# Scale, shift and norm gain folded into two rows per routing, normalised rows kept for the residual, VectorE in place of GpSimd

## The chip, the core and the metric

The kernel runs on one core of a Trainium2 chip. Its engines are TensorE (PE, with a queue of its own for weight loads, PEld), VectorE (DVE), ScalarE (ACT), GpSimd (POOL) and SyncE (SP), which here only issues transfers; ACT and POOL issue some too. Each engine works through its own queue in order and waits on semaphores. The metric is the device time of one launch in microseconds (us), as the median of several runs.

## The reference

Two layers (DEPTH 2) run over 256 latent and 256 context tokens of width 1024; the second layer computes the latent tokens alone. What the change touches is the path from the token mixer's result to the second norm. Cut to that, for each token row:

```
mod = c @ w_ada + b_ada                       # six rows per layer: shift, scale, gate, shift2, scale2, gate2
x1  = layer_norm(alpha*x + gate*mix) * g1 + b1
h2  = x1 * (1 + scale2) + shift2
ffn = moe(h2) = routed experts(h2) + shared expert(h2)
x2  = layer_norm(alpha*x1 + gate2*ffn) * g2 + b2
```

The router takes sigmoid scores of h2 over 64 experts, keeps four groups of eight and the eight best experts of these, and each expert is a SwiGLU network of inner width 256. The shared expert has the same shape.

## The kernel before

Tokens lie in tiles of 128 rows by 1024: four tiles in layer 0, two in layer 1. Matmuls run on operands that are split in a high and a low half: `hilo` (L91, L92) has ACT write the high half and DVE subtract it for the low one (`hb`, `hTl`, `row`). For weights, `whi` is ACT's and `wlo` is DVE's, or POOL's for the share that `split_on_pool` asks for; `raw` is the loaded slab of 1 MB.

A layer has four stages. The **mixer** ends in the merged branches. The **routing** (about 822 to 972 us in layer 0, 2115 to 2229 in layer 1) begins with the out-projection w_o: per tile, matmuls, `yo` and `xr` (L1233, L1234: the gated result added to the residual), the statistics (L560, L561), a chain of tiny DVE instructions for the root (L577 to L583) and the normalised row tile (L570). PE then transposes the tile (L390), ACT applies scale and shift by column (L394), ACT and DVE split it (`hb`), PE computes router logits (L1093, L1094) and the shared expert, and DVE chooses the experts (L1097 to L1122). Beside this, `by_rows` makes the same rows without the transpose, for the experts: the norm's gain (L1182, DVE) and bias (L1183, POOL) give `x1`, which is written to DRAM as x1d; the scale (L1186, DVE) and the shift (L1187, POOL) give `h2`, which is written as h2d. Gain and bias come as two broadcast loads (lng, lnb), scale and shift as `mod` rows that `modulation` has written to DRAM. When the last tile is chosen, DVE writes the list of experts `eid` (L1263); SP reads it and issues the first expert weights w_exp (L129). The **expert stage** gathers rows of h2d and runs the experts. The **post stage** (`post`) loads the shared expert's result yd, the residual x1d, the gate `mod` (m = 5) and the experts' rows y8 on SP's queue; `base` (L1764, L1765) forms alpha*x1 + gate*yd per tile, L1780 to L1787 add the experts' sum, and the second norm follows.

In mixer and routing a scheduler sets the order on each engine: it places instructions by its own estimates of when each engine is free. The expert and the post stage are under `manual_schedule`: there the order is that of the code. In the routing of layer 0, slabs of w_out and w_shared share two `raw` buffers, so a slab can only be loaded when ACT and DVE have split the one two before it.

Of the kernel before, what the change touches and what calls it, by code (L numbers as in the profile page):

```python
# [11 lines left out]
F32 = mybir.dt.float32  # L12
# [3 lines left out]
AF = mybir.ActivationFunctionType  # L16
OP = mybir.AluOpType
# [4 lines left out]
D = 1024  # L22
T = 256
L = 2
# [46 lines left out]
def body(ctx, tc, A, out):  # L71
# [104 lines left out]
    ident = C("ident")  # L176
# [123 lines left out]
    def modulation(chunks, r):  # L300

        n = 2 * len(chunks)
        q = bank("aux", 2)[:, :2 * n].rearrange("p (a b) -> p a b", a=2)
        for i in range(2):
            pe.matmul(q[:, i], r[:, i * 128:i * 128 + 128], C("sel")[:, :n], start=True, stop=True)
        for i, (l, j) in enumerate(chunks):
            m, k0 = j // 4, 2 * (j % 4)
            dve.tensor_tensor(modT[:, l, m, k0:k0 + 2], q[:, :, 2 * i:2 * i + 2],
                              bT_ada[:, l, m, k0:k0 + 2, None].to_broadcast([128, 2, 2]), op=OP.add)
            done[l, m] = done.get((l, m), 0) + 1  # L310
            if m > 1 and done[l, m] == 4:
                p = bank("aux", 2)
                pe.transpose(p[:16, :128], modT[:, l, m].rearrange("p k w -> p (k w)"), ident)
                s = wk.tile([16, 128], F32, name="modr", tag="modr")
                act.activation(s, p[:16, :128], AF.Copy)
                act.dma_start(modrow[l, m].rearrange("w (k c) -> k w c", c=128), s)

    def ada(*chunks):

# [49 lines left out]
    def actt(name):  # L369
        return wk.tile([128, 512], F32, name=name, tag="act", bufs=3)  # L370

    def after_norm(l, m, ln):


        f = wk.tile([128, 2, 8, 2], F32, name="fuse", tag="fuse", bufs=1)
# [667 lines left out]
    def moe(l, merged, x_src):  # L1043
# [6 lines left out]
        with pool_of(f"moe{l}") as K, ExitStack() as es:  # L1050
# [122 lines left out]
                return up, down  # L1173


            gb, bb = bcast(Y, A["ln"][l, 0:1], "lng"), bcast(Y, A["ln"][l, 1:2], "lnb")
            rowm = {}

            def by_rows(t):
                if t % 2 == 0:  # L1180
                    rowm.update({m: mod_b(Y, l, m, t // 2) for m in (4, 3)})
                dve.tensor_tensor(xr[t], xr[t], gb, op=OP.mult)  # L1182
                pool.tensor_tensor(xr[t], xr[t], bb, op=OP.add)  # L1183
                act.dma_start(x1d[t * 128:t * 128 + 128], xr[t])
                h_ = Y.tile([128, D], F32, name="h2")
                dve.tensor_tensor(h_, xr[t], rowm[4], op=OP.mult)  # L1186
                pool.tensor_tensor(h_, h_, rowm[3], op=OP.add)  # L1187
                act.dma_start(h2d[t * 128:t * 128 + 128], h_)
                if gather:
                    hilo(*rowp[t], h_)  # L1190
# [10 lines left out]

            def shared(*tiles):
                if not steps:
                    with split_on_pool(1):
                        steps.extend(dense(A["w_shared"][l], lambda t, k: tuple(z[:, k] for z in h2T[t]), put))
                for t in tiles:
                    steps[0](t)
                    with split_on_pool(1):
                        steps[1](t)

            steps = []
# [538 lines left out]
            with pool_of(f"post{l}") as P:  # L1750
# [7 lines left out]
                if l + 1 < L:  # L1758
                    mod = after_norm(l + 1, 0, 4 * l + 2)

                def base(t):

                    f = sh[t // 2][:, t % 2]
                    dve.tensor_tensor(f, f, g5[t // 2], op=OP.mult)  # L1764
                    dve.scalar_tensor_tensor(xs[t], xs[t], ALPHA, f, op0=OP.mult, op1=OP.add)  # L1765
# [22 lines left out]
                    mv.append(stats(xs[t]))  # L1788
                    ys_.append(root(mv[t]))

                def gain_bias():
                    z = rows2()
                    for i in range(2):
                        sp.dma_start(z[:, i], A["ln"][l, 2 + i:3 + i].to_broadcast([128, D]))
                    return z[:, 0], z[:, 1]

                mv, ys_, yb = [], [], []
                with tc.manual_schedule():
                    if l + 1 < L:
                        w = load(A["w_in"][(l + 1) * 38 + S_RQ])  # L1800
                    for t in range(0, NT, 2):
                        sp.dma_start(sh[t // 2], yd[t * 128:t * 128 + 256].rearrange("(a p) d -> p a d", a=2))
                    for t in range(NT):
                        sp.dma_start(xs[t], x1d[t * 128:t * 128 + 128])
                    g5 = [mod_b(P, l, 5, w_, NS) for w_ in range(NS)]
                    if l + 1 == L:
                        gb, bb = gain_bias()
                    for t in range(NT):
                        base(t)
                    y8v = y8.rearrange("(t p i j) d -> t p i j d", p=128, i=4, j=2)  # L1810
# [2 lines left out]
                        for i in range(4):  # L1813
                            sp.dma_start(yb[t][i], y8v[t, :, i])
                    if l + 1 < L:
                        gb, bb = gain_bias()
                    ln_exp_set()
                    if l + 1 < L:
                        ready[l + 1, S_RQ] = w
# [154 lines left out]
```

## Time and profile before

| | us |
|---|---|
| median of 3 runs | 2800.93 |
| lowest and highest | 2794.92, 2804.31 |
| the profiled execution | 2791.87 |
| its span, first to last instruction | 2790.1 |
| PE busy | 2562.6 (92%) |
| DVE busy | 1645.9 (59%) |
| ACT busy | 1286.5 (46%) |
| POOL busy | 595.5 (21%) |
| mean granted TensorE clock | 0.964 of full |

The profile is that of one execution. "Busy" counts computing instructions alone; the time between an instruction's issue and its start is the idle time that the rows put in brackets, with the instruction that ended it behind the arrow. 1.8 us of the profiled execution's time lie around its span.

### The profile page before, as it was taken

To read this page: it belongs to the slowest core of one execution; us is meant where nothing else is said; L and a number is where in the kernel's file an instruction comes from. 1 tells how busy PE (TensorE), PEld (TensorE's weight loads), DVE (VectorE), ACT (ScalarE), POOL (GpSimd) and SP (SyncE) were. 2 spreads that over 40 slices of the span, in tenths; PEclk is the share of its full clock that TensorE was granted. 3 is DMA by queue.
4 is the path that set the end of the run, shared out by engine and by line. 5 is a ranking of instruction groups with operands and counts; after the bars stand their busy time and mean duration, and the time that the engine had idled before them with its cause. 6 is when DMAs were issued, how large, how long until landed. Compare 5 with 4: busy or idle time off the path is not lost. (4 is left out here: it accounts for less than half of the span.)

```text
span 2790.1 us, 39222 instructions
## 1 busy us (share of the span) xinstructions
PE 2562.6 (92%) x14587; PEld 1846.6 (66%) x14587; DVE 1645.9 (59%) x2968; ACT 1286.5 (46%) x2364; POOL 595.5 (21%) x418
## 2 busy tenths in 40 slices
PE   7999999999997899999999799998989799999995
PEld 6887777788777665555555378887888554554552
DVE  5698895258857654555554577886697622232224
ACT  3434425237852355555555355445475333343331
POOL 2443311222233311212221122213123200000000
PEclk9999999999998899999999899999999799999998
DMA  5221355621152499999999952255325499999996
GB/s 228 72 75 61 106 207 221 231 92 45 61 201 106 171 356 402 408 395 394 402 402 393 358 208 103 95 182 183 120 84 191 163 392 423 422 362 397 419 416 263
DMA packets 118900, 684.09 MB, mean 245 GB/s; under 512 B 21936, under 2 KB 24624, under 8 KB 45744
## 3 DMA queue, kind: packets, MB, share of 16 engines
q1 hardware_dynamic: 92544, 624.80, 57.2%
q0 software_dynamic: 20496, 41.98, 4.0%
q10 hardware_dynamic: 5664, 14.75, 1.4%
q8 instruction: 117, 1.92, 0.3%
q14 instruction: 79, 0.65, 0.1%
HBM read 651.76 MB, written 61.93 MB: 256 GB/s over the span
## 5 line engine op out<-in xcount | busy, mean ns | idle before, releaser
L91 ACT ACTIVATE whi<-raw 128x1024 fp32r<-128x1024 f32 x416 | 428.1, 1053 | 241.1 <-PE mm L231 122.3
L92 DVE TENSOR_TENSOR wlo<-raw,whi 128x1024 fp32r<-128x1024 f32 x305 | 382.8, 1276 | 194.2 <-ACT whi L91 191.0
L231 PE MATMUL mm<-whi,hb 128*128 128x256 f32 (+1 forms) x2016 | 409.6, 300 | 20.2 <-ACT whi L91 5.8
L92 POOL TENSOR_TENSOR wlo<-raw,whi 128x1024 fp32r<-128x1024 f32 x111 | 271.6, 2455 | 639.9 <-ACT whi L91 563.6
L231 PEld LDWEIGHTS mm<-whi,hb 128*128 128x128 f32 x2016 | 334.6, 199 | 28.0 <-issue 7.0
L1578 PE MATMUL mm<-raw,xw 128*64 128x512 f32 x1408 | 331.4, 600 | 0.6 <-DMA raw<-in_w_exp 0.6
L231 PE MATMUL mm<-hb,whi 128*128 128x512 f32 (+1 forms) x1152 | 326.1, 368 | 4.9 <-ACT whi L91 2.9
L231 PE MATMUL mm<-wlo,hb 128*128 128x256 f32 (+1 forms) x1008 | 299.9, 298 | 4.6 <-DVE wlo L92 3.9
L1648 POOL DMA_INDIRECT y<-y,ix x94 | 95.5, 1016 | 974.6 <-ACT y L1644 866.3
L606 DVE SCALAR_TENSOR_TENSOR cacc<-G,cpk,cacc 128x512 f32<-128x512 f32 (+1 forms) x464 | 287.4, 619 | 10.5
L231 PE MATMUL mm<-whi,xp 128*128 128x512 f32 x736 | 262.0, 410 | 1.7 <-ACT whi L91 1.7
L231 PEld LDWEIGHTS mm<-hb,whi 128*128 128x128 f32 x1152 | 206.3, 193 | 41.3 <-issue 4.0
L231 PE MATMUL mm<-hb,wlo 128*128 128x512 f32 (+1 forms) x576 | 212.3, 370 | 9.0 <-DVE wlo L92 8.1
L231 PEld LDWEIGHTS mm<-wlo,hb 128*128 128x128 f32 x1008 | 201.1, 200 | 8.8 <-DVE wlo L92 4.9
L1578 PEld LDWEIGHTS mm<-raw,xw 128*64 128x64 f32 x1408 | 93.9, 136 | 163.9 <-issue 157.5
L231 PE MATMUL mm<-bT,whi 128*128 128x512 f32 (+1 forms) x768 | 194.1, 342 | 5.2 <-ACT bT L91 3.4
L1140 DVE SCALAR_TENSOR_TENSOR hidp<-mm,tab,sgl 128x256 f32<-128x256 f32 x86 | 41.5, 483 | 232.8 <-ACT sgl L1136 232.0
L92 DVE TENSOR_TENSOR xp<-tr,xp 128x512 fp32r<-128x512 f32 (+2 forms) x126 | 59.6, 492 | 194.2 <-ACT xp L91 141.3
L231 PEld LDWEIGHTS mm<-whi,xp 128*128 128x128 f32 x736 | 139.3, 189 | 50.6 <-ACT whi L91 9.4
L1644 ACT ACTIVATE y<-mm 128x512 f32<-128x512 f32 (+1 forms) x188 | 110.1, 594 | 130.5 <-PE mm L1635 69.6
L231 PE MATMUL mm<-wlo,xp 128*128 128x512 f32 x400 | 160.6, 402 | 7.0 <-DVE wlo L92 6.8
L231 PEld LDWEIGHTS mm<-bT,whi 128*128 128x128 f32 x768 | 132.5, 191 | 23.0 <-ACT bT L91 3.7
(652 smaller groups left out, 4468.8 us busy)
## 6 DMA issues: line engine op xcount, KB each, us to landing
raw<-in_w_exp SPq DMA_DIRECT2D x384, 1024.0 KB, 12.4
raw<-in_w_in SPq DMA_DIRECT2D x76, 1024.0 KB, 4.9
raw<-in_w_ada SPq DMA_DIRECT2D x48, 1024.0 KB, 4.9
raw<-in_w_o SPq DMA_DIRECT2D x32, 1024.0 KB, 5.1
yb<-y SPq DMA_DIRECT2D x24, 1024.0 KB, 7.2
mod<-modrow SPq DMA_DIRECT2D x12, 512.0 KB, 8.9
raw<-in_w_shared SPq DMA_DIRECT2D x6, 1024.0 KB, 5.7
x1d<-xr ACTq DMA_DIRECT2D x6, 512.0 KB, 3.2
```

The source lines that it names most:

```text
L91: act.activation(hi, src, AF.Copy)
L92: eng.tensor_tensor(lo, src, hi, op=OP.subtract)
L231: pe.matmul(o, l_, r_, start=start and i == 0, stop=stop and i == len(ops) - 1)
L606: dve.scalar_tensor_tensor(v(y if j == 30 else acc), G[:, :, j:j + T], cpk[:, t, j:j + 1], v(acc), op0=OP.mult, op1=OP.add)
L1140: dve.scalar_tensor_tensor(o[:n], b[:n, 256:512], gate[:n], sg[:n], op0=OP.mult, op1=OP.mult)
L1578: pe.matmul(os_[s][0][half], xhs[s][0](k)[:, half], raws[index[r, i // 2]][:, k % 4 * 512:k % 4 * 512 + 512], start=k == 0, stop=k == 7)
L1644: act.activation(ys[b][:n, c * 512:c * 512 + 512], o[c], AF.Copy)
L1648: pool.indirect_dma_start(out=y8s[s, b][:], in_=ys[b][:n], in_offset=None, out_offset=bass.IndirectOffsetOnAxis(ap=tabs[s][b][1][:n, 1:2], ...
```

## The change

It has four parts.

1. `modulation` writes the rows for m = 3 and m = 4 only when both are there, and writes them already fused with the norm's gain g and bias b: row 4 is g*(1 + scale), row 3 is b*(1 + scale) + shift. Three DVE instructions of 128x16 are added per layer; the number of transposes and row writes stays at four.
2. `by_rows` drops the loads lng and lnb, L1182 and L1183. x1d now receives the normalised rows without gain and bias. h2 is two DVE instructions on the fused rows, where the second was POOL's (L1187).
3. The shared expert's six low halves `wlo` per layer go from POOL to DVE.
4. `post` loads gain and bias of the first norm (gb1, two rows, broadcast) at the head of its loads, moves x1d ahead of yd, and `gained` applies gain and bias to each residual tile: two DVE instructions of 128x1024 per tile, ahead of `base`. In layer 0 gb1 goes into the tile `hx`, in layer 1 into a buffer `yb`.

```diff
-            if m > 1 and done[l, m] == 4:
-                p = bank("aux", 2)
-                pe.transpose(p[:16, :128], modT[:, l, m].rearrange("p k w -> p (k w)"), ident)
...
+            if done[l, m] == 4 and m in (2, 4, 5):
+
+                for i_, z in zip((4, 3), after_norm(l, 3, 4 * l, "fuse2")) if m == 4 else [(m, modT[:, l, m])]:
+                    p = bank("aux", 2)
+                    pe.transpose(p[:16, :128], z.rearrange("p k w -> p (k w)"), ident)
...
-            gb, bb = bcast(Y, A["ln"][l, 0:1], "lng"), bcast(Y, A["ln"][l, 1:2], "lnb")
...
-                dve.tensor_tensor(xr[t], xr[t], gb, op=OP.mult)
-                pool.tensor_tensor(xr[t], xr[t], bb, op=OP.add)
+
                 act.dma_start(x1d[t * 128:t * 128 + 128], xr[t])
                 h_ = Y.tile([128, D], F32, name="h2")
                 dve.tensor_tensor(h_, xr[t], rowm[4], op=OP.mult)
-                pool.tensor_tensor(h_, h_, rowm[3], op=OP.add)
+                dve.tensor_tensor(h_, h_, rowm[3], op=OP.add)
...
-                    with split_on_pool(1):
+                    with split_on_pool(0):
                         steps.extend(dense(A["w_shared"][l], lambda t, k: tuple(z[:, k] for z in h2T[t]), put))
...
+                def gained(t):
+                    for z, op in zip(gb1, (OP.mult, OP.add)):
+                        dve.tensor_tensor(xs[t], xs[t], z, op=op)
...
+                    gb1 = gain_bias(0, hx.rearrange("p (i k) n -> p i (k n)", i=2) if l + 1 < L else rows2())
+                    for t in range(NT):
+                        sp.dma_start(xs[t], x1d[t * 128:t * 128 + 128])
+                        gained(t)
                     for t in range(0, NT, 2):
                         sp.dma_start(sh[t // 2], yd[t * 128:t * 128 + 256].rearrange("(a p) d -> p a d", a=2))
-                    for t in range(NT):
-                        sp.dma_start(xs[t], x1d[t * 128:t * 128 + 128])
                     g5 = [mod_b(P, l, 5, w_, NS) for w_ in range(NS)]
```

The order around it moves at three places. On DVE, routing of layer 0, from the first tile's normalise (`xr<-xr,mv,ny`) on, before:

```order
L570 TENSOR_SCALAR xr<-xr,mv,ny 128x1024
L1182 TENSOR_TENSOR xr<-xr,lng 128x1024
L1233 TENSOR_TENSOR yo<-mm_7893,mod_7680 128x512
L92 TENSOR_TENSOR hb<-h__7816,hb 128x4x128
L1234 SCALAR_TENSOR_TENSOR xr<-xr,yo 128x512
L1186 TENSOR_TENSOR h_8451<-xr,mod_8444 128x1024
L560 BN_STATS bst<-xr 128x6
L92 TENSOR_TENSOR hb<-h__7828,hb 128x4x128
```

And now, with `mod_8444` and `mod_8446` the fused rows:

```order
L572 TENSOR_SCALAR xr<-xr,mv,ny 128x1024
L1186 TENSOR_TENSOR h_8449<-xr,mod_8444 128x1024
L1187 TENSOR_TENSOR h_8449<-h_8449,mod_8446 128x1024
L1233 TENSOR_TENSOR yo<-mm_7893,mod_7680 128x512
L1234 SCALAR_TENSOR_TENSOR xr<-xr,yo 128x512
L92 TENSOR_TENSOR hb<-h__7816,hb 128x4x128
L562 BN_STATS bst<-xr 128x6
L1233 TENSOR_TENSOR yo<-mm_7894,mod_7680 128x512
```

Both h2 instructions of a tile now stand in a row behind its normalise, ahead of the next tile's `yo` and of the low half `hb` for the logits.

On SP, the loads of the same routing (`raw<-in_w_o` are the w_out slabs), before:

```order
L129 DMA raw<-in_w_o 128x2048
L1220 DMA xr<-in_tokens 128x1024
L129 DMA raw<-in_w_o 128x2048 x2
L1078 DMA wr<-in_w_router 128x512
L129 DMA raw<-in_w_o 128x2048
L1220 DMA xr<-in_tokens 128x1024
L129 DMA raw<-in_w_shared 128x2048
L352 DMA lng<-in_ln 128x1024
L352 DMA lnb<-in_ln 128x1024
L1220 DMA xr<-in_tokens 128x1024
L358 DMA mod_8444<-modrow 128x1024
```

And now:

```order
L129 DMA raw<-in_w_o 128x2048
L1220 DMA xr<-in_tokens 128x1024
L129 DMA raw<-in_w_o 128x2048
L1080 DMA wr<-in_w_router 128x512
L1220 DMA xr<-in_tokens 128x1024
L360 DMA mod_8444<-modrow 128x1024
L360 DMA mod_8446<-modrow 128x1024
L129 DMA raw<-in_w_o 128x2048 x2
L1220 DMA xr<-in_tokens 128x1024
L129 DMA raw<-in_w_shared 128x2048 x2
```

lng and lnb are gone, and the last two w_out slabs stand behind a token tile and two `mod` rows. On DVE their low halves, and those of the first two slabs, now follow the mixer's last merges, where they were strewn among them.

On SP, the head of the post stage of layer 0, before:

```order
L1802 DMA yb<-yd 128x2x1024 x2
L1804 DMA x_15185<-x1d 128x1024
L1804 DMA x_15186<-x1d 128x1024
L1804 DMA x_15187<-x1d 128x1024
L1804 DMA x_15188<-x1d 128x1024
L358 DMA mod_15203<-modrow 128x1024
L358 DMA mod_15205<-modrow 128x1024
L1814 DMA yb<-y_165 128x2048 x16
```

And now:

```order
L1797 DMA hx<-in_ln 128x1024 x2
L1807 DMA x_15177<-x1d 128x1024
L1807 DMA x_15178<-x1d 128x1024
L1807 DMA x_15179<-x1d 128x1024
L1807 DMA x_15180<-x1d 128x1024
L1810 DMA yb<-yd 128x2x1024 x2
L360 DMA mod_15205<-modrow 128x1024
L360 DMA mod_15207<-modrow 128x1024
L1820 DMA yb<-y_165 128x2048 x16
```

Two broadcast loads into `hx` stand at the head. The place that `hx` has in SBUF held the hidden operands `hTh` and `hTl` of the last expert unit, so these loads wait for the last matmul that reads `hTl`; before, the head waited for transposes ahead of it.

## Rows read from the trace of the kernel before

**Rows 1.** The page's busy line and its line of transfer rates in 40 slices.

```profile
PE 2562.6 (92%) x14587; PEld 1846.6 (66%) x14587; DVE 1645.9 (59%) x2968; ACT 1286.5 (46%) x2364; POOL 595.5 (21%) x418
...
GB/s 228 72 75 61 106 207 221 231 92 45 61 201 106 171 356 402 408 395 394 402 402 393 358 208 103 95 182 183 120 84 191 163 392 423 422 362 397 419 416 263
```

**Rows 2.** Timeline of POOL, routing 0: start, duration, instruction, count, idle before.

```profile
850.35 2.37 POOL L1183 TENSOR_TENSOR xr<-xr,lnb 128x1024 f32<-128x1024 f32 x1 [25.22 <-DVE xr L1182]
...
886.27 7.02 POOL L92 TENSOR_TENSOR wlo<-raw,whi 128x1024 fp32r<-128x1024 f32 x3 [7.57 <-ACT whi L91]
```

**Rows 3.** Timeline of DVE, routing 0.

```profile
850.23 0.69 DVE L1233 TENSOR_TENSOR yo<-mm,mod 128x512 f32<-128x512 f32 x1
851.02 2.26 DVE L92 TENSOR_TENSOR hb<-h__7816,hb 128x512 fp32r<-128x512 f32 x1
...
886.42 2.35 DVE L1112 TENSOR_TENSOR sel<-sel,gm 128x64 f32<-128x64 f32 x1
...
917.99 0.23 DVE L1112 TENSOR_TENSOR sel<-sel,gm 128x64 f32<-128x64 f32 x1
...
926.33 0.69 DVE L92 TENSOR_TENSOR hb<-h__8421,hb 128x512 fp32r<-128x512 f32 x1
...
927.27 2.03 DVE L377 TENSOR_TENSOR fuse<-modT,lnT 128x16 f32<-128x16 f32 x1
```

**Rows 4.** Instructions of a line grouped by form: count, busy us, mean ns, idle before.

```profile
L1187 POOL TENSOR_TENSOR h<-h,mod 128x1024 f32<-128x1024 f32 x6 | 15.0, 2503 | 13.5 <-DVE h L1186 11.4 <-ACT hb L91 2.1
...
L1182 DVE TENSOR_TENSOR xr<-xr,lng 128x1024 f32<-128x1024 f32 x6 | 7.4, 1226 | 6.8 <-PE tr L390 6.8
```

**Rows 5.** One line's instructions: count, ns minimum/median/maximum, first and last start.

```profile
L92 DVE TENSOR_TENSOR wlo<-raw,whi x305: 1209/1224/3365, 38.2 to 2717.5; 128x1024 fp32r<-128x1024 f32 x153
...
L92 POOL TENSOR_TENSOR wlo<-raw,whi x111: 2328/2401/3388, 40.1 to 2180.9; 128x1024 fp32r<-128x1024 f32 x111
```

**Rows 6.** Waits of all engines, 820 to 946 us: waiter and releaser, us, times, longest.

```profile
PE aux L1094 <- DVE hb L92: 10.5, 6, 4.2
...
PE tr L390 <- DVE xr L570: 7.4, 3, 6.7
```

**Rows 7.** Windows, routing 0: length, busy us of PE, PEld, DVE, ACT, POOL, granted clock, DMA share, GB/s.

```profile
880.00:900.00 20.00, 13.30 (x84) 13.09 (x85) 15.48 (x46) 6.64 (x14) 7.83 (x4) 0.76 0.28 102
...
920.00:940.00 20.00, 18.57 (x98) 15.07 (x97) 9.88 (x29) 10.51 (x22) 5.17 (x2) 1.00 0.26 106
```

**Rows 8.** Timelines of DVE and SP, end of routing 0.

```profile
945.71 0.21 DVE L1263 CAST eid<-aux 1x64 int32<-1x64 f32 x1 [0.51 <-PE aux L1262]
...
948.72 11.03 SPq L129 DMA_DIRECT2D raw<-in_w_exp  x7
```

**Rows 9.** Timeline of DVE, routing 1.

```profile
2156.11 1.18 DVE L1234 SCALAR_TENSOR_TENSOR xr<-xr,yo 128x256 f32<-128x256 f32 x1
...
2193.25 2.22 DVE L1113 TENSOR_SCALAR gm<-gm 128x8 f32<-128x8 f32 x1
```

**Rows 10.** Timelines of SP, PE and DVE, head of the post stage of layer 0.

```profile
1563.41 0.90 SPq L1802 DMA_DIRECT2D yb<-yd  x2
...
1567.06 0.40 PE L231 MATMUL mm<-whi,hTl 128*128 128x512 f32 x1
...
1580.40 1.23 DVE L1764 TENSOR_TENSOR yb<-yb,mod 128x1024 f32<-128x1024 f32 x1 [15.61 <-DMA mod<-modrow]
...
1588.84 1.22 DVE L1765 SCALAR_TENSOR_TENSOR x<-x,yb 128x1024 f32<-128x1024 f32 x1
...
1591.51 2.29 DVE L1780 TENSOR_TENSOR yb<-yb 128x2048 f32<-128x2048 f32 x1 [1.44 <-DMA yb<-y]
```

**Rows 11.** Windows, post stage of layer 0, columns as in rows 7.

```profile
1580.00:1590.00 10.00, 5.95 (x8) 2.58 (x9) 9.47 (x8) 0.00 (x0) 0.00 (x0) 0.51 1.01 425
```

**Rows 12.** Timeline of DVE, post stage of layer 1.

```profile
2751.28 1.22 DVE L1765 SCALAR_TENSOR_TENSOR x<-x,yb 128x1024 f32<-128x1024 f32 x1 [0.21 <-DVE yb L1764]
2762.66 2.29 DVE L1780 TENSOR_TENSOR yb<-yb 128x2048 f32<-128x2048 f32 x1 [10.15 <-DMA yb<-y]
```

More of the change, by code (lines that the diff above doesn't have):

```diff
@@ L310, in modulation @@
             done[l, m] = done.get((l, m), 0) + 1
-            if m > 1 and done[l, m] == 4:
-                p = bank("aux", 2)
-                pe.transpose(p[:16, :128], modT[:, l, m].rearrange("p k w -> p (k w)"), ident)
-                s = wk.tile([16, 128], F32, name="modr", tag="modr")
-                act.activation(s, p[:16, :128], AF.Copy)
-                act.dma_start(modrow[l, m].rearrange("w (k c) -> k w c", c=128), s)
+            if done[l, m] == 4 and m in (2, 4, 5):
+                for i_, z in zip((4, 3), after_norm(l, 3, 4 * l, "fuse2")) if m == 4 else [(m, modT[:, l, m])]:
+                    p = bank("aux", 2)
+                    pe.transpose(p[:16, :128], z.rearrange("p k w -> p (k w)"), ident)
+                    s = wk.tile([16, 128], F32, name="modr", tag="modr")
+                    act.activation(s, p[:16, :128], AF.Copy)
+                    act.dma_start(modrow[l, i_].rearrange("w (k c) -> k w c", c=128), s)
     def ada(*chunks):
@@ L370, in actt, with after_norm @@
         return wk.tile([128, 512], F32, name=name, tag="act", bufs=3)
-    def after_norm(l, m, ln):
-        f = wk.tile([128, 2, 8, 2], F32, name="fuse", tag="fuse", bufs=1)
+    def after_norm(l, m, ln, name="fuse"):
+        f = wk.tile([128, 2, 8, 2], F32, name=name, tag=name, bufs=1)
         g, b = (lnT[:, ln + i, :, None].to_broadcast([128, 8, 2]) for i in range(2))
@@ L1207, in shared @@
                     steps[0](t)
-                    with split_on_pool(1):
+                    with split_on_pool(0):
                         steps[1](t)
@@ L1789, in summed, with gain_bias @@
                     ys_.append(root(mv[t]))
-                def gain_bias():
-                    z = rows2()
+                def gain_bias(n, z):
                     for i in range(2):
-                        sp.dma_start(z[:, i], A["ln"][l, 2 + i:3 + i].to_broadcast([128, D]))
+                        sp.dma_start(z[:, i], A["ln"][l, n + i:n + i + 1].to_broadcast([128, D]))
                     return z[:, 0], z[:, 1]
@@ L1800, in moe @@
                         w = load(A["w_in"][(l + 1) * 38 + S_RQ])
+                    gb1 = gain_bias(0, hx.rearrange("p (i k) n -> p i (k n)", i=2) if l + 1 < L else rows2())
+                    for t in range(NT):
+                        sp.dma_start(xs[t], x1d[t * 128:t * 128 + 128])
+                        gained(t)
                     for t in range(0, NT, 2):
                         sp.dma_start(sh[t // 2], yd[t * 128:t * 128 + 256].rearrange("(a p) d -> p a d", a=2))
-                    for t in range(NT):
-                        sp.dma_start(xs[t], x1d[t * 128:t * 128 + 128])
                     g5 = [mod_b(P, l, 5, w_, NS) for w_ in range(NS)]
                     if l + 1 == L:
-                        gb, bb = gain_bias()
+                        gb, bb = gain_bias(2, rows2())
                     for t in range(NT):
@@ L1815, in moe @@
                     if l + 1 < L:
-                        gb, bb = gain_bias()
+                        gb, bb = gain_bias(2, rows2())
                     ln_exp_set()
```

## The prediction

> **What bounds the kernel now.** I read the page first: TensorE is busy for 2562.6 us, 92% of the span, GpSimd for 595.5 [rows 1]. So GpSimd's work as such is worth nothing, and the change can only act where TensorE stands still. The line of transfer rates shows two long stretches at about 400 GB/s [rows 1]: the two expert stages. In the first (slices 15 to 22) the rate never leaves 356 to 408, so it is bound by transfers; whatever lets it begin earlier moves all of it. What lets it begin is the list of experts: `eid` is written at 945.71 and the first expert weights are issued at 948.72 [rows 8]. Therefore the routing, from the out-projection to `eid`, is serial time, and I looked there next.
>
> In the waits of that stretch TensorE stands 10.5 us for the low half of the logits' operand and 7.4 us for the normalised tile [rows 6], both VectorE's. VectorE is then what paces the tiles, and its timeline shows why: many of its instructions are several times too long. The low half `hb` takes 2.26 us at 851.02 and 0.69 at 926.33; the 128x64 product L1112 takes 2.35 at 886.42 and 0.23 at 917.99; a fused row of 16 elements takes 2.03 at 927.27 [rows 3]. Beside each of them GpSimd is running a two-input instruction: its bias L1183 from 850.35 to 852.72, three `wlo` from 886.27 to 893.29 [rows 2]. VectorE does not slow down evenly, it stands until GpSimd's instruction is over. From 851.02 to 927.27 there are 11 such instructions (the first, one of the middle and the last are in rows 3), and what each takes beyond the undisturbed time of its own line adds up to 20.7 us. In the second routing there are 10, from 2156.11 (1.18 us) to 2193.25 (2.22 us) [rows 9], with 16.1 us.
>
> The Trainium skill ("SBUF — State Buffer", Who interferes with whom) says that VectorE and GpSimd share a port pair that is locked for a whole instruction, and that only VectorE instructions with two SBUF inputs, or in a two-port mode, are held by it. The trace agrees: `yo`, one input of which comes from PSUM, takes 0.69 us at 850.23 beside a running GpSimd instruction [rows 2, 3]. By that rule the most that 14 GpSimd instructions (8 of the rows, 6 `wlo`) could take from VectorE in the first routing is 14 x 2.4 = 34 us, which would make its gain 34 - 7.3 - 2.7 = 24 us instead of the 10.7 below; the 20.7 us that the rows show are what I use.
>
> **Routing, layer 0.** Removed from GpSimd: 4 biases, 4 shifts and 6 `wlo`, all of those in the stretch that do the damage. So the 20.7 us go. Per tile VectorE loses the gain L1182 (1.23 us [rows 4]) and gets the shift, which I price like L1182, since shape and operands are alike: nothing in sum. It gets 6 `wlo` at 1.22 [rows 5]: 7.3 us, 4 of them inside the chain of the third tile, 2 in that of the fourth. GpSimd's shift took 2.50 [rows 4] and the row write behind it comes earlier, which nobody on the path waits for. What is lost at the start: the low halves of w_out move behind the last merges and slabs 2 and 3 are loaded later, behind a tile and two rows. Following the new order with undisturbed durations, I get the first tile's normalise at about 850.6, against 847.9 before: +2.7 us, with the matmuls of the second tile filling a part of TensorE's wait. Sum: -20.7 + 7.3 + 2.7 = **-10.7 us**. The bounds: if the last tile's wait for GpSimd's bias and TensorE's lower clock also go, -16, which is where my walk through all four tiles ends (last logits about 920 instead of 936). If only the late start counts and TensorE paces the tiles, +3. I take the sum, because TensorE's waits for VectorE [rows 6] come to 17.9 us, so most of the stretch had to be paid there, but hardly all.
>
> The granted clock is 0.76 of full between 880 and 900, where TensorE is busy for 13.3 of 20 us, and 1.00 between 920 and 940, where it is busy for 18.6 [rows 7]. The Trainium skill ("TensorE: Matmul & The Clock Gate", Part 1) says that the throttled state is the default and sustained activity releases it. By that, shorter waits would also give back clock: an estimate from rows 7 is 13.3 x 0.24 = 3.2 us in such a window, which would make the sum about -14; I leave it out since waits remain at every tile.
>
> **Routing, layer 1.** The same parts: -16.1 us of stretch and + 6 x 1.22 = 7.3 of `wlo`, four of which stand in the first tile's chain where they took VectorE's time already by stretching it. That is -8.8. I take **-7**, because the excess between the first and the last `wlo` there falls partly into waits for transposes; bounds +2 (the `wlo` on the path, the stretch not) and -10.
>
> **Post stage, layer 0.** Before, the first load was issued at 1563.41 [rows 10], when the transposes of the last unit were through. Now gb1 goes into `hx`, and must wait for the last matmul that reads `hTl`, at 1567.06 + 0.40 = 1567.5 [rows 10]. SP's queue is in order, so x1d, yd, the gate rows and y8 all stand behind it: 4.1 us late. And the stream in front of y8 grows by two 512 KB rows, 1.05 MB, which at the 425 GB/s of that stretch [rows 11] is 2.5 us. The end of the first wait is a transfer (L1780 at 1591.51 <- yb<-y [rows 10]), so both count: **+6.6 us**, the experts' sum starting near 1598. The eight `gained` instructions are 8 x 1.22 = 9.8 us (priced like L1182) and lie in the 15.6 us that VectorE stands idle before 1580.40 [rows 10]; `base` would then run from about 1584.6 for 9.7 us to 1594.3, before y8 is there. If that cover were gone, up to 9.8 us more would show, as the later y8 loads reuse buffers that `base` reads. Bounds: +2.5 (the bytes alone) and +10.
>
> **Post stage, layer 1.** gb1 takes the early place of yd and waits for much the same; x1d goes as before, yd comes after it. `base` ends at 2752.50 and VectorE then stands 10.15 us for y8 [rows 12]: two tiles of `gained`, 4.9 us, and a yd that is some 2.5 us later fit in. The extra megabyte lies partly in idle transfer time: **+0.7**, bounds 0 and +3.
>
> **Nothing.** The six fused instructions on 128x16 are made while the modulation is being computed under the mixer's matmuls; uncovered, at the 0.23 us of an undisturbed 128x64 product [rows 3], they would be 1.4 us. Two broadcast loads per layer leave the routings, whose transfers run at 102 to 106 GB/s [rows 7].
>
> Together: -10.7 - 7 + 6.6 + 0.7 = **-10.4 us**. The profiled execution took 2791.87 us, so it would take 2781.5; its time is 9 us below the median of 2800.93, within the spread of the three runs. Against the median: **2790.5 us**.
>
> **Rivals.** *TensorE and ScalarE pace the tiles* as much as VectorE: only half of the relief shows, -5.4 - 3.5 + 7.3 = -1.6 us, 2799.3. For it: behind each normalise come transposes, ScalarE's scale, split and logits, which nobody shortens. Against it: the 17.9 us of waits for VectorE [rows 6].
>
> *The `wlo` cost more than GpSimd's stretch did.* They now stand in VectorE's queue inside the chains of the normalise, and what they wait for holds the root, the next `hb` and so TensorE; GpSimd stood 7.57 us for ScalarE's `whi` ahead of 886.27 [rows 2], and VectorE would stand there instead. It decides as soon as less than (7.3 + 2.7) / 20.7 = 48% of the stretch was on the path. With a quarter: -5.2 + 10 = +4.8, in layer 1 -4 + 7.3 = +3.3, and the post stages +7.3: +15.4, 2816. Against it: `whi` is ScalarE's, which is idle for most of the routing (6.64 of 20 us [rows 7]).
>
> *The expert stage does not follow.* If it were paced by tiles coming free and not by the first load, the routings' gain would be lost again, and the post stages alone give +7.3, 2808. Against it: 400 GB/s throughout [rows 1].
>
> **How the numbers follow.** The forecast (-4 to -18) has 0.55, the first rival 0.25, the second 0.12, the third 0.08. 0.3%, 8.4 us, is about what a measurement of this kernel can tell from no change. Of the forecast's cases some five in six lie beyond it: faster 0.47. Within 0.3%: the rest of the forecast, the first rival and most of the third, 0.39. Slower: 0.14, of it the second rival. For the range I add the low bounds in part (-16 - 8 + 5 = -19, or 2782, and 2 for the spread of the median) and go up to the third rival: 2780 to 2808.
>
> **What would show it.** In the new profile: `hb` and L1112 in the routings at 0.69 and 0.23 throughout; `eid` near 935 and, after the shift of layer 0, the second routing shorter by about 7; the first gb1 load at 1567.5 less the gain, and the experts' sum 6.6 us later against the last matmul. It would be wrong if TensorE's waits for L570 stay, if VectorE is seen waiting for `whi` inside the chains, or if the late w_out slabs cost more than 2.7 us.

## The result and the profile after

The changed kernel takes 2766.8 us, the median of 5 runs (2763.7 to 2771.9); the kernel before, beside it, 2800.9 (2794.9 to 2804.7). The ratio is 0.9892, with a 95% interval of 0.9877 to 0.9907: by the ratio 30 us faster, by the two medians 34, where 10.4 were forecast. The time lies 13 us below the range. Two later groups of runs gave 0.9874 (0.9854 to 0.9895) and 0.9892 (0.9875 to 0.9909) for the same kernel.

The profiled executions are 2790.1 and 2761.9 us long, 28.2 apart. Where that came from shows at six places (start of the instruction, for the matmul its end, us):

| place | before | after | gained so far |
|---|---|---|---|
| first normalise of routing 0 (L570, now L572) | 847.05 | 846.88 | 0.2 |
| `eid` of routing 0 | 945.71 | 917.54 | 28.2 |
| end of the last `hTl` matmul of the expert stage | 1567.46 | 1541.07 | 26.4 |
| first sum of the experts' rows, post stage 0 | 1591.51 | 1571.01 | 20.5 |
| `eid` of routing 1 | 2209.38 | 2177.25 | 32.1 |
| first sum, post stage 1 | 2762.66 | 2734.11 | 28.6 |

So the first routing gave 28 us, the post stage of layer 0 took 5.9 back, and 11.6 came up to the second `eid`. Of these, 8.2 lie within the second routing (from its first normalise to `eid`: 44.1 us before, 35.9 now) and 3.4 in the mixer ahead of it (573.7 us from the sum to that normalise before, 570.3 now; two further executions of the changed kernel took 572.4 and 574.4, so this part is within their spread). The expert stages gave nothing: the first is 1.8 us longer, and from the second `eid` to the last sum the changed kernel needs 3.6 us more (4.1 and 5.3 in the two further executions).

The first rows are VectorE's and GpSimd's timeline in the first routing of the changed kernel, the answers to [rows 2] and [rows 3]:

```profile
851.46 0.69 DVE L92 TENSOR_TENSOR hb<-h__7816,hb 128x512 fp32r<-128x512 f32 x1
...
873.89 0.22 DVE L1114 TENSOR_TENSOR sel<-sel,gm 128x64 f32<-128x64 f32 x1
...
878.70 1.83 DVE L1120 CAST mb<-m 128x64 bf16<-128x64 f32 x1
...
917.54 0.21 DVE L1263 CAST eid<-aux 1x64 int32<-1x64 f32 x1 [0.73 <-PE aux L1262]
```

```profile
878.63 1.86 POOL L1478 MEMSET raw<- 128x1024 f32 x2 [56.22 <-DVE wlo L92]
891.86 1.85 POOL L1478 MEMSET raw<- 128x1024 f32 x2 [11.37 <-DVE wlo L92]
```

The same `hb` that took 2.26 us takes 0.69, the same product 0.22 instead of 2.35. From the first normalise on GpSimd has nothing left in the stretch but clearings of memory, and one of them still holds VectorE, a cast of 64 columns that takes 1.83 us.

Now the window from 820 us to `eid`, before and after: length, busy us of PE, PEld, DVE, ACT and POOL with instructions, granted clock, DMA share, GB/s.

```profile
820.00:945.70 125.70, 101.33 (x620) 91.47 (x619) 88.80 (x231) 40.27 (x77) 40.51 (x20) 0.86 0.32 115
```

```profile
820.00:917.50 97.50, 87.87 (x610) 79.73 (x609) 78.17 (x239) 41.58 (x77) 6.59 (x7) 0.96 0.40 146
```

TensorE stood still for 24.4 us before and for 9.6 now, 14.7 less; and for nearly the same matmuls (620 and 610) it was busy 13.5 us less, at a granted clock of 0.96 instead of 0.86. Its waits for VectorE in the stretch, in the form of [rows 6]:

```profile
PE tr L392 <- DVE xr L572: 2.9, 4, 1.9
...
PE aux L1096 <- DVE hb L92: 1.0, 2, 0.9
```

The two that came to 17.9 us come to 3.9.

### The profile page after: what moved, and what is told of

Read it like the earlier page. It is cut to its first block, busy times and chain, and to the rows that moved or that the text cites. A ratio compares the mean times of both kernels' runs of the same rounds, so it can differ in the third digit from the quotient of the medians.

```text
span 2761.9 us, 39210 instructions
## 1 busy us (share of the span) xinstructions
PE 2549.9 (92%) x14587; PEld 1832.7 (66%) x14587; DVE 1631.9 (59%) x2998; ACT 1287.3 (47%) x2364; POOL 538.1 (19%) x394
## 5 line engine op out<-in xcount | busy, mean ns | idle before, releaser
L92 DVE TENSOR_TENSOR wlo<-raw,whi 128x1024 fp32r<-128x1024 f32 x317 | 395.8, 1270 | 186.3 <-ACT whi L91 182.6
L231 PE MATMUL mm<-whi,hb 128*128 128x256 f32 (+1 forms) x2016 | 399.9, 295 | 21.3 <-ACT whi L91 10.2
L92 POOL TENSOR_TENSOR wlo<-raw,whi 128x1024 fp32r<-128x1024 f32 x99 | 243.8, 2470 | 611.6 <-ACT whi L91 512.4
L231 PEld LDWEIGHTS mm<-whi,hb 128*128 128x128 f32 x2016 | 327.0, 195 | 28.9 <-ACT whi L91 11.1
```

Of the source, the lines that this page charges most:

```text
L92: eng.tensor_tensor(lo, src, hi, op=OP.subtract)
L231: pe.matmul(o, l_, r_, start=start and i == 0, stop=stop and i == len(ops) - 1)
```

## The experiments

Theory A: VectorE is held by GpSimd's two-input instructions, and TensorE behind it; taking them away is nearly all of the gain. Theory B: the new order (late slabs, matmuls of the second tile ahead of the first tile's transposes) is a large part of it. The third, from the prediction: `wlo` on VectorE cost more than on GpSimd. All changes are to the changed kernel unless said otherwise; kernels that were measured in one group share the runs of the kernel before.

**The shift back on GpSimd.**

```diff
-                dve.tensor_tensor(h_, h_, rowm[3], op=OP.add)
+                pool.tensor_tensor(h_, h_, rowm[3], op=OP.add)
```

> The changed kernel (2766.8 us, 34.1 below the kernel before), with the shift that makes h2 (L1187) back on GpSimd: six two-input instructions of 2.4 us there, six of 1.22 us fewer on VectorE. The order of the loads and of TensorE's matmuls in the routings stays the new one. Theory A, VectorE held by GpSimd's two-input instructions, and TensorE behind it, made the time: each such instruction costs about 28 us / 14 = 2 us in the first routing of before, so here some +2 us for each of the six, less a little for the VectorE time saved: +6 to +12 us, 2773 to 2779. Theory B, the new order (matmuls of the second tile ahead of the first tile's transposes, late slabs) made the time: within 3 us of the changed kernel, since the order is kept.

2778.5 us, ratio 0.9937 (0.9924 to 0.9950): six instructions on GpSimd cost 12 us, although VectorE was spared six of its own. The order of the slabs and of TensorE's matmuls is the new one; theory A.

**The shared expert's low halves back on GpSimd.**

```diff
-                    with split_on_pool(0):
+                    with split_on_pool(1):
...
-                    with split_on_pool(0):
+                    with split_on_pool(1):
```

> The changed kernel with the shared expert's twelve low halves wlo back on GpSimd, six per routing, so twelve instructions of 2.4 us there and twelve of 1.22 us fewer on VectorE. Theory A (VectorE held by GpSimd): +10 to +20 us, 2777 to 2787, and tiny VectorE instructions of 2 us beside each wlo on GpSimd. Theory B (the new order): 0 or a few us less than the changed kernel, since VectorE has 14.7 us less work in the chains of the routings. The second theory of the prediction, that wlo on VectorE costs more than on GpSimd, expects -5 to -10 us.

2780.9 us, ratio 0.9935 (0.9920 to 0.9950), some 12 us more. The third theory, -5 to -10, falls. VectorE's and GpSimd's timelines show what is meant by holding:

```profile
871.49 2.40 DVE L1111 TENSOR_SCALAR gm<-gm 128x8 f32<-128x8 f32 x1
...
873.92 2.33 DVE L1114 TENSOR_TENSOR sel<-sel,gm 128x64 f32<-128x64 f32 x1
...
876.29 2.21 DVE L1115 TENSOR_SCALAR gm<-gm 128x8 f32<-128x8 f32 x1
```

```profile
871.47 7.00 POOL L92 TENSOR_TENSOR wlo<-raw,whi 128x1024 fp32r<-128x1024 f32 x3 [49.38 <-DVE gm L1110]
```

Three `wlo` in a row on GpSimd, and three instructions on 8 or 64 columns take 2.2 to 2.4 us each: in 7 us VectorE does next to nothing.

**Both back on GpSimd.** The two edits above together.

> The changed kernel with both returned to GpSimd, the shift (six instructions) and the shared expert's low halves (twelve): 18 of the 24 GpSimd instructions that the change took away, in the new order. If what each costs adds up, +12 and +13 us from the two kernels with one of them give +25 us, about 2791, and eid of the first routing 16 us later than in the changed kernel. If they hide behind one another (VectorE held by either while TensorE waits anyway), less than +20.

2788.9 us, ratio 0.9962 (0.9947 to 0.9977), 23 us above the changed kernel of the same group (2765.6). In total the costs add up. In the first routing they do not quite: it takes 14 us longer, where 16 were expected.

**GpSimd work that nobody waits for.**

```diff
                 act.dma_start(x1d[t * 128:t * 128 + 128], xr[t])
+                spare = Y.tile([128, D], F32, name="spare")
+                for m in (4, 3):
+                    pool.tensor_tensor(spare, xr[t], rowm[m], op=OP.add)
```

> The changed kernel with two extra GpSimd additions of 128x1024 per tile of the routings, twelve in all, from the normalised tile and a modulation row into a spare tile that nothing reads: GpSimd work that no engine waits for. With the spare tile the scheduler goes back to the old order of the w_out slabs in the first routing. Theory A (VectorE held by GpSimd): twelve instructions of 2.4 us at some 2 us each, +15 to +25 us, 2782 to 2792. Theory B (order): the old order returns and its gain in the first routing goes, +20 us or more, the same time, but with the stretched VectorE instructions not mattering: it is told from theory A by the next kernel, which has the old order without GpSimd. A theory that GpSimd's results were waited for (rows late, not VectorE held): 0 us.

2804.3 us, ratio 1.0021 (1.0010 to 1.0032): twelve additions that no engine reads undo the whole change. Against the kernel with the old order further down, which has the same instructions in the same order on VectorE and TensorE without them, `eid` of the first routing is 27 us later (946.8 against 919.8); eight of the twelve stand there. VectorE's timeline and GpSimd's there:

```profile
847.09 1.23 DVE L1189 TENSOR_TENSOR h<-xr,mod 128x1024 f32<-128x1024 f32 x1
848.35 3.30 DVE L1190 TENSOR_TENSOR h<-h,mod 128x1024 f32<-128x1024 f32 x1
851.57 0.68 DVE L1236 TENSOR_TENSOR yo<-mm,mod 128x512 f32<-128x512 f32 x1
852.28 2.13 DVE L1237 SCALAR_TENSOR_TENSOR xr<-xr,yo 128x512 f32<-128x512 f32 x1
```

```profile
847.13 6.73 POOL L1187 TENSOR_TENSOR spare<-xr,mod 128x1024 f32<-128x1024 f32 x2 [24.68 <-DVE xr L572]
```

The holding goes both ways: GpSimd's addition takes 3.4 us here, against 2.4 where VectorE leaves it alone, and `yo`, with one input from PSUM, keeps its 0.68 between two held neighbours.

**The kernel before with nothing changed but the engine.** (Edits to the kernel before; gain and bias stay in the routings.)

```diff
-                pool.tensor_tensor(xr[t], xr[t], bb, op=OP.add)
+                dve.tensor_tensor(xr[t], xr[t], bb, op=OP.add)
...
-                pool.tensor_tensor(h_, h_, rowm[3], op=OP.add)
+                dve.tensor_tensor(h_, h_, rowm[3], op=OP.add)
...
-                    with split_on_pool(1):
+                    with split_on_pool(0):
```

> The kernel before with only the engine changed: the bias L1183, the shift L1187 and the shared expert's twelve wlo on VectorE instead of GpSimd. Nothing is fused, gain and bias are applied in the routings, the post stages are those of before, and the first routing keeps the old order of its w_out slabs. Theory A (VectorE held by GpSimd): the routings lose the stretch but pay 2 x 1.22 us more per tile than the changed kernel, six tiles, at most 15 us; against before -39 us of routings' gain + 7 to 15 = -24 to -32 us, 2769 to 2777. Theory B (order): only a little of the gain of the first routing, about -10 us, 2791.

2771.3 us, ratio 0.9910 (0.9897 to 0.9924): 25 of the 30 us, with more work on VectorE than before, in the old order of the slabs, without fusing anything. Theory A. All the rest of the change together is worth the other 5 us, less than the two intervals can tell apart. `eid` of the first routing stands at 928.76:

```profile
928.76 0.21 DVE L1263 CAST eid<-aux 1x64 int32<-1x64 f32 x1 [0.73 <-PE aux L1262]
```

**The old order, GpSimd empty.**

```diff
                 act.dma_start(x1d[t * 128:t * 128 + 128], xr[t])
+                spare = Y.tile([128, D], F32, name="spare")
+                pool.memset(spare[:, 0:8], 0.0)
```

> The changed kernel with one more tile of 4 KB per partition in the routings, of which GpSimd clears eight columns per token tile (writes only). Its only effect is that the scheduler goes back to the old order of the w_out slabs in the first routing, with GpSimd still out of the way. Theory A (VectorE held by GpSimd is nearly all of the gain): 2766 to 2771, eid of the first routing near 918 to 922 us. Theory B (the order is a large part): eid near 928 us, as in the kernel before with its GpSimd work on VectorE, and 2775 or more.

2769.6 us, ratio 0.9900 (0.9884 to 0.9917), `eid` at 919.8. The first routing takes 1 to 2 us longer than the changed kernel's; the times themselves cannot be told apart. Theory B falls. Only the order of the slabs is the old one here: the order of TensorE's matmuls among the tiles still differs from the kernel before.

**More work on VectorE.** The scale of h2 issued twice, and four times.

```diff
                 dve.tensor_tensor(h_, xr[t], rowm[4], op=OP.mult)
+                dve.tensor_tensor(h_, xr[t], rowm[4], op=OP.mult)
```

> The changed kernel with the scale instruction of h2 (L1186) issued twice per tile: six more VectorE instructions of 1.22 us in the routings, 4.9 us in the first and 2.4 in the second, and none on GpSimd. It prices VectorE's own time there, to be held against the price of GpSimd's instructions (six of them gave +12 us in the kernel with the shift on GpSimd, where VectorE was even spared 7.3 us). If VectorE's time paces the routings one to one: +7 us, 2774. If a part is hidden: +2 to +5 us. If any delay on VectorE is multiplied through TensorE's clock: +10 us or more.

2773.1 us, ratio 0.9921 (0.9903 to 0.9939), 3 to 7 us above the three medians of the changed kernel (2765.6 to 2770.0) for 7.3 us on VectorE, with an interval that overlaps two of theirs; the first routing shows 1 to 2 of its 4.9.

> The changed kernel with the scale instruction of h2 issued four times per tile: 18 more VectorE instructions of 1.22 us, 14.7 us in the first routing and 7.3 in the second, none on GpSimd. That is about the VectorE time that GpSimd's instructions took from the first routing net (20.7 - 7.3 = 13.4 us), but here the scheduler knows of it. If delay on VectorE is multiplied by TensorE's falling clock whatever its source: eid of the first routing some 25 us later than in the changed kernel (917.5 to 921.4), and mean granted clock there under 0.90. If it counts one to one: 15 us later. If the scheduler can put what it knows of beside other work: under 8 us.

2782.0 us, ratio 0.9940 (0.9919 to 0.9962). In the first routing 14.7 us more of VectorE's time moved `eid` to 926.09, which is 9 us later, counted from the first normalise. The 25 us of the first theory did not come. But TensorE's clock falls here too, with GpSimd empty. The windows of this kernel, in the columns used above:

```profile
860.00:880.00 20.00, 19.52 (x163) 19.00 (x162) 19.90 (x54) 8.56 (x16) 1.03 (x2) 1.00 0.47 153
880.00:900.00 20.00, 16.07 (x78) 13.09 (x76) 19.28 (x63) 10.93 (x19) 2.66 (x3) 0.91 0.15 59
```

```profile
820.00:926.10 106.10, 94.04 (x612) 84.48 (x613) 88.75 (x250) 44.08 (x79) 5.25 (x6) 0.90 0.36 130
```

From 820 us to `eid` the granted clock is 0.90, where the changed kernel had 0.96, and TensorE is busy for 94.0 us instead of 87.9 with nearly the same matmuls (612 and 610): 6.2 of the 8.6 us by which the window is longer. The clock falls where TensorE begins to stand: 1.00 up to 880, where it is busy for 19.5 of 20 us, 0.91 up to 900 (16.1 us), and 0.74 from 900 to 920 (17.2 us). So a delay on VectorE can cost clock without any work on GpSimd. The scheduler knows of these instructions and could put matmuls beside them; that this is why they cost less per us than GpSimd's is not shown.

The first routing of all these kernels, from the start of the first normalise to the start of `eid`, with the time that TensorE stands in it and its granted clock:

| kernel | GpSimd two-input instructions | VectorE's own work against the changed kernel | us | TensorE stands, us | clock |
|---|---|---|---|---|---|
| before | 14 of 2.4 us | -7.3 | 98.7 | 19.4 | 0.88 |
| changed (three executions) | 0 | 0 | 70.7, 71.9, 71.8 | 4.2, 4.0, 4.0 | 1.00, 0.98, 0.98 |
| old order | 0 | 0 | 72.8 | 3.5 | 1.00 |
| scale twice | 0 | +4.9 | 72.9 | 5.4 | 1.00 |
| before, on VectorE | 0 | +9.8 | 79.7 | 6.4 | 0.96 |
| scale four times | 0 | +14.7 | 80.5 | 7.8 | 0.92 |
| shift on GpSimd | 4 of 2.4 us | -4.9 | 81.0 | 7.7 | 0.92 |
| low halves on GpSimd | 6 of 2.4 us | -7.3 | 79.6 | 10.4 | 0.94 |
| both on GpSimd | 10 of 2.4 us | -12.2 | 85.6 | 11.9 | 0.88 |
| spare additions | 8 of 3.3 us | 0 | 100.6 | 16.8 | 0.83 |

With the old order of the slabs (before, old order, before on VectorE, spare additions) 480 to 482 matmuls lie in this stretch, with the new one 456 to 458, so a kernel is best held against one of its own order. VectorE's own work costs 0.3 to 0.7 us per us. If I take 0.6 (9.1 / 14.7, the scale four times), a GpSimd instruction costs (25.9 + 4.4) / 14 = 2.2 us before, 3.1 for the shift, 2.1 for the low halves, 2.1 for both, and (100.6 - 72.8) / 8 = 3.5 for the spare ones: about the whole time that it runs. This is an estimate, as the 0.6 comes from one kernel; without any credit for VectorE's own work the five are 1.8, 2.4, 1.4, 1.4 and 3.5. The clock goes roughly with TensorE's standing and not with GpSimd as such: the scale four times and the shift on GpSimd leave it standing equally long, at the same clock.

**The head of the post stage: gain and bias behind the other loads.**

```diff
-                    gb1 = gain_bias(0, hx.rearrange("p (i k) n -> p i (k n)", i=2) if l + 1 < L else rows2())
                     for t in range(NT):
                         sp.dma_start(xs[t], x1d[t * 128:t * 128 + 128])
-                        gained(t)
                     for t in range(0, NT, 2):
                         sp.dma_start(sh[t // 2], yd[t * 128:t * 128 + 256].rearrange("(a p) d -> p a d", a=2))
+                    gb1 = gain_bias(0, hx.rearrange("p (i k) n -> p i (k n)", i=2) if l + 1 < L else rows2())
+                    for t in range(NT):
+                        gained(t)
```

> The changed kernel, but at the head of the post stages gain and bias of the first norm (gb1) are loaded behind the residual tiles x1d and yd instead of ahead of them, and the additions that use them follow. If the head of SP's queue, waiting for the last matmul of the experts, is what makes the post stage of layer 0 5.9 us longer than before, some 4 us of it return (the part that is the later start; the part that is the extra megabyte stays): 2760 to 2764 against 2766.8, the first sum of the experts' rows 4 us earlier after the last matmul. If the stage is bound by bytes or by VectorE's additional instructions: within 1 us of the changed kernel.

2776.1 us, ratio 0.9924 (0.9911 to 0.9938): a miss. SP's head starts 4 us earlier and the first sum comes 31.5 us after the last matmul, not 26. VectorE's timeline says why the sum is not earlier:

```profile
1552.75 1.23 DVE L1763 TENSOR_TENSOR x<-x,hx 128x1024 f32<-128x1024 f32 x1 [14.88 <-DMA hx<-in_ln]
...
1570.94 1.23 DVE L1769 SCALAR_TENSOR_TENSOR x<-x,yb 128x1024 f32<-128x1024 f32 x1
1572.09 2.28 DVE L1784 TENSOR_TENSOR yb<-yb 128x2048 f32<-128x2048 f32 x1
```

Gain and bias now come last, VectorE waits 14.9 us for them, and then its 19 us of `gained` and `base` set the end, with no wait ahead of the sum: the cover for the eight instructions was gone. This explains 1.6 us against the changed kernel (29.9), not the 9 by which the median is longer: the profiled execution was the fastest of its five (2767.2 us) and shows the rest at no place, so its cause stays open.

**Gain and bias early, in a weight buffer.**

```diff
-                    gb1 = gain_bias(0, hx.rearrange("p (i k) n -> p i (k n)", i=2) if l + 1 < L else rows2())
+                    p_, n_ = buffer("raw")
+                    gb1 = gain_bias(0, p_.tile([128, 2048], F32, name="raw", tag="raw", bufs=n_).rearrange("p (i n) -> p i n", i=2) if l + 1 < L else rows2())
```

> The changed kernel, with gain and bias of the first norm in layer 0's post stage loaded into a buffer of the expert weights, which comes free well before the last matmul, instead of into hx. Nothing else moves: SP's head waits as in the kernel before, and VectorE has gain and bias before the residual tiles land. If the late head (+4.1 us) and the extra megabyte (+2.5) are the whole of the 5.9 us that the post stage of layer 0 lost, 4 us return: first sum of the experts' rows 26 to 27 us after the last matmul (29.9 in the changed kernel, 24.1 before), 2762 to 2764 where the changed kernel has 2766.8. If VectorE's additional instructions set the end, as in the kernel with gb1 behind: within 1 us of the changed kernel.

2774.8 us, ratio 0.9914 (0.9896 to 0.9932), 9 us above the changed kernel beside it: a miss in the time, a hit at its place. The first sum comes 23.6 us after the last matmul (1568.60 against 1545.01), as before the change (24.1). But SP's timeline shows one slab of the next mixer's weights loaded ahead where the changed kernel loads two, and from the first sum to the first normalise of the second routing it takes 583.8 us, against 570.3 to 574.4 in the three executions of the changed kernel. That the late slab is the reason is not shown: no kernel changes it alone, and this stretch took up to 579.6 us in a kernel that loads two ahead (that with the merges' low halves, below):

```profile
1526.73 0.36 SPq L129 DMA_DIRECT2D raw<-in_w_in  x1
1527.20 0.83 SPq L1797 DMA_DIRECT2D raw<-in_ln  x2
1541.02 1.75 SPq L1808 DMA_DIRECT2D x<-x1d  x4
...
1591.89 24.18 SPq L129 DMA_DIRECT2D raw<-in_w_in  x4
```

**The gain early, the bias behind.**

```diff
+                        gb1 = (P.tile([128, D], F32, name="g1"), hx[:, 0:8].rearrange("p k n -> p (k n)")[:, 0:D])
+                        sp.dma_start(gb1[0], A["ln"][l, 0:1].to_broadcast([128, D]))
...
+                        sp.dma_start(gb1[1], A["ln"][l, 1:2].to_broadcast([128, D]))
+                        for z, op in zip(gb1, (OP.mult, OP.add)):
+                            for t in range(NT):
+                                dve.tensor_tensor(xs[t], xs[t], z, op=op)
```

> The changed kernel with the head of layer 0's post stage split: the gain row of the first norm goes into a free 4 KB tile and is loaded first, the residual tiles and yd follow, and only the bias row goes into hx, behind them; VectorE multiplies the four tiles first and adds the bias later. No buffer of the weights is touched, which the kernel with gb1 early paid for in the next mixer. If the wait of SP's head for the last matmul is what the post stage of layer 0 lost, the first sum of the experts' rows comes 26 to 27 us after the last matmul of the experts (29.8 in the changed kernel, 24.1 before) and the time is 3 us below the changed kernel. If VectorE's additions set the end: as the changed kernel.

> The changed kernel once more, on the same chip as the two others, for their comparison: 0.987 to 0.990 of the kernel before.

2766.1 us (ratio 0.9875, 0.9856 to 0.9895) against 2770.0 for the changed kernel beside it (0.9892, 0.9875 to 0.9909). At its place it does what was expected, the first sum 26.5 us after the last matmul against 29.9; the 3.9 us between the medians are of that size, but the intervals overlap, and the changed kernel reached 2765.6 in another group. In the traces the gain at the place is lost again in the mixer: the second routing's first normalise starts at 2147.38, in the changed kernel beside it at 2147.93. A gain in time is not shown.

```profile
1526.38 0.38 SPq L1807 DMA_DIRECT2D g<-in_ln  x1
1539.73 1.75 SPq L1809 DMA_DIRECT2D x<-x1d  x4
1541.53 1.21 SPq L1811 DMA_DIRECT2D yb<-yd  x2
1543.76 0.34 SPq L1812 DMA_DIRECT2D hx<-in_ln  x1
```

**The merges' low halves on VectorE too** (on top of gain and bias behind).

```diff
-                with weight_pool(f"w_merge{l}", *((2, 3), (0, 0))[l]), split_on_pool(3):
+                with weight_pool(f"w_merge{l}", *((2, 3), (0, 0))[l]), split_on_pool(0):
```

> The kernel with gb1 behind, and besides the low halves wlo of the mixers' merges (one in three there) on VectorE instead of GpSimd. If the same holding of VectorE by GpSimd costs time where TensorE is already busy without waits, some 5 us less than the kernel with gb1 behind; if VectorE's stretched instructions are hidden behind TensorE there, no change, within 2 us.

2776.4 us, ratio 0.9932 (0.9917 to 0.9946), against 2776.1 without it: no change. The edit takes 21 low halves off GpSimd. In layer 0's merges, from 340 to 580 us, TensorE is busy for 239 of 240 us at full clock without it: where TensorE has matmuls enough and does not wait for VectorE, GpSimd's hold on VectorE costs nothing that can be measured.

**The changed kernel a second time.**

> The changed kernel itself once more, beside the others on the same chip, so that they can be held against it directly: about 0.989 of the kernel before, and eid of the second routing some 28 to 32 us earlier than in the kernel before, which tells how much of the second routing's gain is spread between executions.

2765.6 us, ratio 0.9874 (0.9854 to 0.9895). Its second `eid` stands at 2180.97, 3.7 us later than in the first profile, and that of the changed kernel's third profile at 2183.63, 6.4 later. So of the differences in the table of places, some 6 us in the second layer are the spread between executions.

## Why the prediction was wrong

**What held.** The mechanism and its place: the routing is serial up to `eid`, VectorE paces its tiles, and GpSimd's two-input instructions hold VectorE. All three rivals fell: more than half of the relief showed, as TensorE's waits for VectorE went from 17.9 to 3.9 us; the low halves are cheaper on VectorE (putting them back cost 12 us alone, and 7 to 10 on top of the shift, and in the first routing VectorE waits for no `whi` between the first normalise and `eid`); and the expert stage followed the first load (28.2 us at `eid`, 26.4 at the last matmul). The post stage of layer 0 was forecast at +6.6 and took 5.9: 4.1 by its head, which starts right behind the last matmul, and 1.8 from the head to the first sum (28.1 us before, 29.9 now), where 2.5 were put down for the bytes:

```profile
1541.10 0.80 SPq L1797 DMA_DIRECT2D hx<-in_ln  x2
...
1550.77 40.21 SPq L1820 DMA_DIRECT2D yb<-y  x16
```

```profile
1548.78 9.67 DVE L1763 TENSOR_TENSOR x<-x,hx 128x1024 f32<-128x1024 f32 x8 [10.39 <-DMA x<-x1d]
...
1568.22 1.23 DVE L1769 SCALAR_TENSOR_TENSOR x<-x,yb 128x1024 f32<-128x1024 f32 x1
1571.01 2.29 DVE L1784 TENSOR_TENSOR yb<-yb 128x2048 f32<-128x2048 f32 x1 [1.57 <-DMA yb<-y]
```

That its cover was thin was said there; the 1.57 us in front of the sum are what was left of it, and the kernel with gain and bias behind used them up. The second routing (-7) gained 8.2. Post stage 1 (+0.7) has its first sum 21.6 to 22.7 us after the last matmul on `hT`, 21.2 before: +0.4 to +1.5. The second expert stage is 3.0 to 3.8 us longer in the three executions; no term of the forecast covers that, and its cause stays open.

**The step that failed** is the size of the first routing's term, -10.7. From the first normalise to `eid` 27 to 28 us came; counted from the end of the mixer's last merge matmul, so that the late start is in it, 24 to 26 (123.3 us before; 97.1, 99.2 and 99.3 in the three executions). Two steps of the sum made it too small:

The clock, put at nothing. By the windows, 14.7 us of the 28.2 are time in which TensorE no longer stands, which is near the 13.4 of my sum without the late start. The other 13.5 are TensorE's busy time for nearly the same matmuls, at a granted clock of 0.96 instead of 0.86. I had that part in the text, at 3.2 us for one window of 20, beside the rule of the Trainium skill ("TensorE: Matmul & The Clock Gate", Part 1) that the throttled state is the default and activity releases it, and set it aside because waits would remain at every tile; at 3.9 us instead of 17.9 they hardly did. The runs agree that the clock goes with the waits: the scale four times, with GpSimd empty, brought TensorE's standing and the clock back together (7.8 us, 0.92). No kernel here changes the clock and leaves the waits as they are.

The price of a GpSimd instruction. I added up what 11 VectorE instructions took beyond their undisturbed time, 20.7 us, 1.5 us for each of GpSimd's 14. By the table of routings each costs about its whole duration, 2.1 to 3.5 us, the lost clock included. What I weighed against it and left out of the range was nearer: the Trainium skill ("SBUF — State Buffer", Who interferes with whom) gives the lock for the whole instruction, and 14 x 2.4 us with the same `wlo` and late start made the gain 24 us. The rows agree with the Trainium skill there as to which instructions are held: `yo` with its PSUM input never is (at most 0.69 us in ten), the small `TENSOR_SCALAR`, the cast and those with two SBUF inputs are. The sum of the stretched rows was a lower bound: it counts what the held instruction loses, not what TensorE loses behind it. In the other direction, `wlo` at its full 7.3 us was too dear: VectorE's own work costs 0.3 to 0.7 us per us here.

The late slabs were not the error. I charged 2.7 us; from the end of the last merge matmul to the first normalise it takes 24.6 us before and 26.5 to 27.4 now, 1.8 to 2.8 more. That the first normalise starts 0.2 us earlier in the table of places is due to the mixer, which ended 2.0 us earlier in that execution. The slabs' order makes little of it, as the kernel with the old order and GpSimd empty takes 26.8.

**The range** took its low end from the walk through the new order (-16), although TensorE's lower clock was meant to be gone there; why that walk came out 8 to 10 us short is not shown. It should have reached to the bound of 24 us that stood in the text.

## What to carry to other kernels

Where GpSimd runs two-input instructions beside a chain of small VectorE instructions that TensorE waits for, price each at its whole GpSimd time, not at the stretch that single rows show, and move it to VectorE at half that time even though VectorE is the engine that paces. Where the matmul engine's waits nearly vanish, count its clock as well: here that was as much as the waits themselves. Where TensorE has work enough of its own, as in the merges here, the same move is worth nothing. A load put at the head of an in-order queue takes over the wait of the tile that it is put in; before it is moved, look what its late arrival does to the work that it was covering, and whether what is gained there is still there at the next stage.

## What the runs showed of the hardware that I had not expected

GpSimd clearing memory, which reads nothing, holds VectorE too: the cast at 878.70 took 1.83 us instead of 0.20, beside a clearing from 878.63 to 880.49, and another at 913.87 took 0.82 beside a clearing from 913.68 to 914.63. The instructions with two SBUF inputs are not held by clearing: beside the one from 891.86 to 893.71, `gs<-top` (128x8) took 0.17 us, as in a tile without clearing. And the holding is mutual: the spare additions took up to 3.43 us, with 2.35 as the shortest:

```profile
L1187 POOL TENSOR_TENSOR spare<-xr,mod x12: 2349/3218/3432, 847.1 to 2201.1; 128x1024 f32<-128x1024 f32 x12
```
